# First mixer of a two-layer block: denser S5 tables, scans and rotations in fewer instructions, and a new order around them

## The chip, the cores and the metric

One Trainium2 chip, one core. The kernel runs a whole two-block network on 512 tokens of width 1024 in float32. The metric is the device time of one execution in microseconds; of several runs the median counts.

## The reference, cut to what matters

The first block has a mixer of two halves that share one projection, `proj = rms_norm(x) @ w_in`. The change lies in this mixer alone; what follows it (its feed-forward part, dilated attention, a squared-relu MLP, HGRN2 and another MLP) stays as it is.

```python
# S5: 32 groups of 16 inputs, 64 complex states each, over L = 512 steps
dt = exp(log_dt); mag = exp(lr * dt); ar, ai = mag * cos(li * dt), mag * sin(li * dt)
fr, fi = ((ar - 1) * lr + ai * li) / den, (ai * lr - (ar - 1) * li) / den
bbar_re, bbar_im = fr * b_re - fi * b_im, fr * b_im + fi * b_re
x[t] = (ar + i ai) * x[t-1] + bbar @ u[t]                 # associative_scan
y = einsum(xr, c_re) - einsum(xi, c_im) + d * u           # then gelu and a GLU
# attention: 8 query heads, 2 key heads of 64, window 128, sink
q, k = partial_rotary(q), partial_rotary(k)               # the first 16 of 64
# x1 * cos - x2 * sin, x2 * cos + x1 * sin, with x1, x2 of 8 each
```

## The kernel before, in words

**Arithmetic.** Every large product is made of three matmuls on split operands (`mm3`, L260 to L262): a weight tile of 128x1024 is loaded to `wst`, ACT copies its high part to `whi` (L183) and DVE subtracts to get `wlo` (L184). Splits are made ahead by `K.ws.more` and `take`. Every engine runs its instructions in the order in which the program emits them.

**S5 in chunks of four.** Time is cut into 128 chunks of 4 steps. A state has 64 values for each of two groups on the 128 partitions, and 16 such pairs of groups lie along the free axis. Four tables are made from the parameters: `tC`, `tS` (cosine and sine of 4m times the state's angle, m = 0 to 127) by doubling, n = 1, 2, ... 64, each doubling with a complex product (`cmul`, L945 to L950) and a squaring of the phase; `TP` (L996 to L1013: b times powers of a, the first half on DVE, the second on POOL); `CA` (L1024 to L1032: c times powers of a, on POOL). They are kept with zero blocks, so that a pair of groups is one matmul: b and c come from memory already padded from 16 to 32 columns, and every instruction on them runs over the zeros as well.

For each of four quarters f, `s5_in` multiplies the chunked inputs with `Pm` (transposed `TP`), rotates by the tables, runs eight scans of 128 elements on DVE (L1124) with the decay `r4` broadcast, and rotates back; DVE and POOL share these steps. `s5_kb` builds the part inside a chunk, `s5_y` the outputs, `s5_z` brings them back to the order of time with 32-column matmuls (L1171). `make_up` (L1048) is a similar rearrangement of the inputs.

**Attention.** `qkv` projects keys and values, then queries, in six pairs of token blocks. After each pair ACT evacuates and six DVE instructions rotate (L1220 to L1225), then PE transposes. `scores`, `normalize` and `values` follow.

**Order.** The angles (`angles`, L803 on) are emitted between the norms of the third and the fourth token block. Then come the splits of two u tiles, the u projection with the steps of `early` (TP, then tables) between its parts, and then the two strings `_MIX_INNER` and `_MIX_OUTER`, which list the remaining steps in order of emission: `e` a step of `early`, `CA0`/`CA1` a step of `make_CA`, `inF` of `s5_in`, `qkv`, `scT`, `yF`, `zF` and so on.

Of the kernel before, what the change touches and what calls it, by code (L numbers as in the profile page):

```python
# [210 lines left out]
_MIX_INNER = """e e CA0 e u qkv in0 qkv qkv in0 qkv in0 in1 qkv CA0 qkv in1 qkv Pm2 qkv CA0 CA0 in1 Pm3 qkv qkv qkv in2 in2  # L211
CA0 qkv xT in2 in3 kb0 qkv in3 sc0 qkv y0 CA1 sc1 sc0 CA1 CA1 sc0 sc1 in3 kb1 sc1 n0 tab v0 CA1 v0 n1 CA1 v0
# [16 lines left out]
class Kern:  # L229
# [573 lines left out]
    def angles(self, pool, th, n, cos, sin):  # L803

        K, nc = self, self.nc
        k = pool.tile([128, n], F32, name="ang_k")
# [7 lines left out]
        nc.scalar.activation(sin, th, AF.Sin)  # L814
        nc.scalar.activation(cos, k, AF.Sin)

    def mix(self, ctx):
# [25 lines left out]
        inv = load("c_inv8", [128, 8], q=G)  # L843
        get_xin(1)
# [5 lines left out]
        b_in = load("s5_b", [128, 2, 16, 32], pool)  # L850
        CAs, CI = [pool.tile([128, 2, 8, 5, 32], F32, name="CA")], {}

        def get_c(h, q):
            t = CI[h] = pool.tile([128, 2, 8, 32], F32, name="qk", bufs=3)
            q.dma_start(t, K.ins["s5_c"][:, :, 8 * h:8 * h + 8])

        get_c(0, nc.sync)
# [37 lines left out]
        G.tensor_tensor(dt, e16, prm[:, 2], op=OP.pow)  # L895
# [7 lines left out]
        G.tensor_scalar(lr, prm[:, 0], -1e-4, 0.0, op0=OP.min, op1=OP.add)  # L903
        G.tensor_mul(t16[0], lr, dt)
# [3 lines left out]
        square(3)  # L908
        V.tensor_copy(posf, pos_i)
# [3 lines left out]
        K.angles(c_, th, 48, cs[:, 0], cs[:, 1])  # L913
# [3 lines left out]

        prenorm(3)
# [34 lines left out]
        tb2 = K.xp.tile([128, 2, 16, 128], F32, name="x")  # L953
        tC, tS = tb2[:, 0], tb2[:, 1]
        e4 = [c_.tile([128, 16], F32, name=f"e4_{i}") for i in range(6)]
        ph = [[c_.tile([128, 16], F32, name=f"ph{n}_{i}") for i in range(2)] for n in range(2)]
        cmul(G, G, e4[0], e4[1], c1, s1_, c1, s1_, e4[2:])
        cmul(G, G, ph[0][0], ph[0][1], e4[0], e4[1], e4[0], e4[1], e4[2:])
# [3 lines left out]
        G.memset(tC[:, :, 0:1], 1.0)  # L962
        G.memset(tS[:, :, 0:1], 0.0)
        tmp = [pool.tile([128, 4, 128], F32, name=f"wt{i}") for i in range(4)]

        def tables():
            n = 1
            while n < 128:
                pr_, pi_ = ph[0]
                for o in range(0, n, 32):  # L970
                    w = min(n, 32)
                    bc = [p[:, :, None].to_broadcast([128, 16, w]) for p in (pr_, pi_)]
                    t = [t.rearrange("p a b -> p (a b)")[:, 0:16 * w].rearrange("p (g m) -> p g m", g=16) for t in tmp]
                    cmul(V, G if n > 4 else V, tC[:, :, n + o:n + o + w], tS[:, :, n + o:n + o + w],
                         tC[:, :, o:o + w], tS[:, :, o:o + w], bc[0], bc[1], t)
                    if n >= 16:
                        yield
                n *= 2
                if n < 128:
                    cmul(V, V, ph[1][0], ph[1][1], pr_, pi_, pr_, pi_, e4[2:])  # L980
                    ph.reverse()

        def b8(t, h):
            return t[:, None, 8 * h:8 * h + 8, None].to_broadcast([128, 2, 8, 32])

        TPs = {}

        def make_TP0():

            TP = TPs[0] = pool.tile([128, 2, 8, 4, 32], F32, name="TP")  # L990
            t1, t2 = (tmp[i].rearrange("p q (g m) -> p (q g) m", m=32).rearrange("p (c q) m -> p c q m", c=2)
                      for i in range(2))
            for j in (3, 2, 1, 0):
                a = b_in[:, :, 0:8] if j == 3 else TP[:, :, :, j + 1]
                yr, yi = (fr, fi) if j == 3 else (ar, ai)
                V.tensor_mul(t1, a, b8(yr, 0))  # L996
                V.tensor_mul(t2, a, b8(yi, 0))
                V.tensor_sub(TP[:, 0, :, j], t1[:, 0], t2[:, 1])
                V.tensor_add(TP[:, 1, :, j], t1[:, 1], t2[:, 0])
                yield  # L1000
            G.tensor_copy(b_in[:, :, 0:8], TP[:, :, :, 3])

        def make_TP1():

            TP = TPs[1]
            for j in (3, 2, 1, 0):
                a = b_in[:, :, 8:16] if j == 3 else TP[:, :, :, j + 1]
                yr, yi = (fr, fi) if j == 3 else (ar, ai)
                for c in range(2):
                    o = TP[:, c, :, j]  # L1010
                    G.tensor_mul(o, a[:, c], b8_(yr, 1))
                    G.tensor_mul(cat, a[:, 1 - c], b8_(yi, 1))
                    (G.tensor_add if c else G.tensor_sub)(o, o, cat)  # L1013
            G.tensor_copy(b_in[:, :, 8:16], TP[:, :, :, 3])

        cat = pool.tile([128, 8, 32], F32, name="cat")
        def b8_(t, h):
            return t[:, 8 * h:8 * h + 8, None].to_broadcast([128, 8, 32])

        def make_CA(h):  # L1020

            CA = CAs[h]
            c = CI.pop(h)
            G.tensor_copy(CA[:, 0, :, 0], c[:, 0])  # L1024
            G.tensor_scalar(CA[:, 1, :, 0], c[:, 1], -1.0, 0.0, op0=OP.mult, op1=OP.add)
            yield
            for n in range(4):
                for c in range(2):
                    o = CA[:, c, :, n + 1]
                    G.tensor_mul(o, CA[:, c, :, n], b8_(ar, h))  # L1030
                    G.tensor_mul(cat, CA[:, 1 - c, :, n], b8_(ai, h))
                    (G.tensor_sub if c else G.tensor_add)(o, o, cat)  # L1032
                yield
# [27 lines left out]
        def early():  # L1061
            yield from make_TP0()
# [12 lines left out]
        e = step(e)  # L1075
        K.transposes(xin[:, 3, :], xT, 3)
        e = step(e)
        u_half(2, 0)
        e = step(e)
        X = pool.tile([128, 2, 4, 4, 128], F32, name="X")  # L1080
        TPs[1] = X[:, :, 2:4].rearrange("p c f q (j h) -> p c (f q) j h", j=4)
        make_TP1()
# [54 lines left out]
        def s5_kb(f):  # L1137
# [5 lines left out]
            for q in range(4):  # L1143
                for j in range(4):
                    o = p[32 * j:32 * j + 32, q, 32 * j:128]
# [704 lines left out]
```

## Time and profile before

| | us |
|---|---|
| median of 3 runs (2193.4 to 2195.33) | 2195.24 |
| the profiled execution | 2195.75 |
| its span, first to last instruction | 2194.0 |
| PE busy in the span | 2117.1 (96%) |
| DVE busy | 1247.6 (57%) |
| ACT busy | 778.1 (35%) |
| POOL busy | 304.0 (14%) |

The span is the time from the first instruction to the last; the execution has 1.75 us around it. PE is the tensor engine, DVE the vector engine, ACT the scalar engine, POOL the general one. Shares over the whole span hide stages: the mixer takes roughly the first 300 us. A wait is idle time of an engine, put down to the instruction that ended it. The times of matmuls overlap, since they are pipelined; so do those of other engines by a little.

### The profile page before, as it was taken

How to read it: one execution, taken by the hardware profiler on the slowest of the kernel's cores; microseconds unless marked ns; L12 is line 12 of the kernel's file. 1: busy time of each engine (PE TensorE's matmuls, PEld its weight loads, DVE VectorE, ACT ScalarE, POOL GpSimd, SP SyncE). 2: the span in 40 equal slices, each digit the busy share in tenths (PEclk: the TensorE clock that was granted, in tenths of full speed). 3: DMA queues.
4: the chain of work that ended last, by engine and by line, in shares of the span. 5: the costliest groups of instructions: out<-in, count | busy, mean ns of one | idle time of the engine just before them, and what ended most of it. 6: DMA issues, size and time to landing. Idle time of an engine off the chain costs nothing.

```text
span 2194.0 us, 31487 instructions
## 1 busy us (share of the span) xinstructions
PE 2117.1 (96%) x12708; PEld 1772.8 (81%) x12708; DVE 1247.6 (57%) x2236; ACT 778.1 (35%) x1433; POOL 304.0 (14%) x366
## 2 busy tenths in 40 slices
PE   7779999999999999999999999999999999999997
PEld 6767788888888888888887888888898878888885
DVE  8986453334366666666666644444556556444444
ACT  4135443222223444424443433222254534322331
POOL 7660100000003212122220100000110001000001
PEclk9879999999999999999999999999999999999998
DMA  4200233223225333233332232223222222222321
GB/s 142 70 25 30 106 125 96 92 81 115 96 68 191 112 111 116 82 112 108 95 111 102 87 115 96 96 77 109 103 84 82 79 78 85 96 96 81 112 96 68
DMA packets 64994, 210.00 MB, mean 96 GB/s; under 512 B 10528, under 2 KB 15280, under 8 KB 64848
## 3 DMA queue, kind: packets, MB, share of 16 engines
q1 hardware_dynamic: 55808, 181.32, 24.4%
q0 software_dynamic: 6896, 20.08, 3.2%
q10 hardware_dynamic: 2144, 6.58, 0.9%
q8 instruction: 100, 1.64, 0.3%
q14 instruction: 46, 0.38, 0.1%
HBM read 186.97 MB, written 4.19 MB: 87 GB/s over the span
## 4 chain that ended last, share of the span: by engine, by line
PE 59%; issue 24%; DVE 2%; POOL 1%; ACT 1%; DMA 0%; POOLq 0%; ACTq 0%; DVEq 0%
PE mm L260 14%; PE mm L261 13%; PE mm L262 13%; PE dn L371 4%; PE dn L370 4%; PE dn L372 4%; PE o L734 1%; PE dn L657 1%; POOL rv L306 1%; POOL rr L308 1%; PE dn L711 1%; PE dn L713 1%; ACT P L641 0%; DVE wlo L184 0%; PE dn L744 0%
## 5 line engine op out<-in xcount | busy, mean ns | idle before, releaser
L260 PE MATMUL mm<-xh,whi 128*128 128x512 f32 (+1 forms) x1488 | 566.7, 381 | 3.0 <-ACT xh L312 3.0
L261 PE MATMUL mm<-xl,whi 128*128 128x512 f32 (+1 forms) x1488 | 558.1, 375 | 3.3 <-DVE xl L313 3.1
L262 PE MATMUL mm<-xh,wlo 128*128 128x512 f32 (+1 forms) x1488 | 557.5, 375 | 1.3 <-DVE wlo L184 1.3
L184 DVE TENSOR_TENSOR wlo<-wst,whi 128x1024 fp32r<-128x1024 f32 x328 | 441.2, 1378 | 130.4 <-ACT whi L183 129.5
L183 ACT ACTIVATE whi<-wst 128x1024 fp32r<-128x1024 f32 x328 | 331.7, 1049 | 372.0 <-PE dn L371 221.9
L260 PEld LDWEIGHTS mm<-xh,whi 128*128 128x128 f32 x1488 | 282.1, 190 | 60.9 <-issue 7.3
L262 PEld LDWEIGHTS mm<-xh,wlo 128*128 128x128 f32 x1488 | 282.3, 190 | 52.7 <-DVE wlo L184 1.5
L261 PEld LDWEIGHTS mm<-xl,whi 128*128 128x128 f32 x1488 | 282.3, 190 | 52.2 <-DVE xl L313 4.5
L371 PE MATMUL dn<-whi,hl 128*128 128x512 f32 x688 | 271.6, 395 | 0.0
L370 PE MATMUL dn<-whi,hh 128*128 128x512 f32 x688 | 271.0, 394 | 0.1
L372 PE MATMUL dn<-wlo,hh 128*128 128x512 f32 x688 | 268.6, 390 | 0.0
L260 PE MATMUL mm<-whi,xh 128*128 128x256 f32 x608 | 179.4, 295 | 4.5 <-DVE kT L1188 4.5
L261 PE MATMUL mm<-wlo,xh 128*128 128x256 f32 x608 | 173.8, 286 | 3.2 <-DVE wlo L184 3.2
L262 PE MATMUL mm<-whi,xl 128*128 128x256 f32 x608 | 173.6, 286 | 0.0
L480 DVE SCALAR_TENSOR_TENSOR x<-x,dn 128x512 f32<-128x512 f32 x112 | 75.6, 685 | 169.1 <-PE dn L372 169.1
L306 POOL TENSOR_SCALAR rv<-ss 128x1 f32<-128x1 f32 (+1 forms) x42 | 26.8, 638 | 1037.7 <-ACT junk L348 440.4
L370 PEld LDWEIGHTS dn<-whi,hh 128*128 128x128 f32 x688 | 129.4, 188 | 30.4 <-DVE x L341 0.5
L372 PEld LDWEIGHTS dn<-wlo,hh 128*128 128x128 f32 x688 | 129.4, 188 | 29.2
L371 PEld LDWEIGHTS dn<-whi,hl 128*128 128x128 f32 x688 | 129.6, 188 | 26.7
L260 PEld LDWEIGHTS mm<-whi,xh 128*128 128x128 f32 x608 | 118.1, 194 | 12.7 <-issue 7.5
L261 PEld LDWEIGHTS mm<-wlo,xh 128*128 128x128 f32 x608 | 118.4, 195 | 3.5 <-DVE wlo L184 3.4
L262 PEld LDWEIGHTS mm<-whi,xl 128*128 128x128 f32 x608 | 118.2, 194 | 0.0
(403 smaller groups left out, 2646.9 us busy)
## 6 DMA issues: line engine op xcount, KB each, us to landing
wst<-in_wstream SPq DMA_DIRECT2D x328, 512.0 KB, 3.5
qks<-qkT POOLq DMA_DIRECT2D x96, 128.0 KB, 2.7
v<-gb SPq DMA_DIRECT2D x128, 32.0 KB, 1.8
X<-in_x SPq DMA_DIRECT2D x4, 512.0 KB, 7.7
xn<-in_x POOLq DMA_DIRECT2D x4, 512.0 KB, 4.6
x_d<-x POOLq DMA_DIRECT2D x4, 512.0 KB, 8.9
x<-x_d POOLq DMA_DIRECT2D x4, 512.0 KB, 7.4
out<-x SPq DMA_DIRECT2D x4, 512.0 KB, 2.6
```

Source lines behind the costliest of these rows:

```text
L183: K.nc.scalar.activation(hi, t, AF.Copy)
L184: K.nc.vector.tensor_sub(lo, t, hi.bitcast(F32))
L260: mm(ps, wh, xh, start=first, stop=False, skip_group_check=True)
L261: mm(ps, wh, xl, start=False, stop=False, skip_group_check=True)
L262: mm(ps, wl, xh, start=False, stop=last, skip_group_check=True)
L306: self.nc.gpsimd.tensor_scalar(v[:, :n], ss, scale, eps, op0=OP.mult, op1=OP.add)
L308: self.nc.gpsimd.tensor_tensor(r[:, :n], v[:, :n], self.nhalf[:, :n], op=OP.pow)
L370: mm(p, hT[i][0][:, c], w[i][0][:, n], start=i == 0, stop=False)
L371: mm(p, hT[i][1][:, c], w[i][0][:, n], start=False, stop=False)
L372: mm(p, hT[i][0][:, c], w[i][1][:, n], start=False, stop=i == m - 1)
L480: nc.vector.scalar_tensor_tensor(x, x, ALPHA if first else 1.0, ps, op0=OP.mult, op1=OP.add)
L657: mm(s, q[r, 0, c], q[r, 1, keys], start=True, stop=True)
```

## The change

- b and c come unpadded (16 columns). `TP` is made for both halves at once on DVE in a small buffer, and ACT copies each power into the padded tables; `CA` stays on POOL with half the elements, and ACT copies it at the end. The padded tables are zeroed by memsets first.
- The tables for m = 0 to 15 and the phases 64, 128 and 256 come from angles directly: one product with a constant, one call of `angles` on 16x19 elements, and Sin on ACT. Only n = 16, 32 and 64 are doubled.
- The norms of all four blocks now come first; POOL's power for dt, and all angles, follow.
- `s5_in` runs two scans of 512 elements, with a decay table `R_tab` (made by ACT) that has zeros where a new row of 128 begins.
- The rotation takes four instructions instead of six, with a table `rot` that ACT fills (its sine part once negated).
- `s5_kb` and `s5_z` emit their matmuls so that successive ones write different groups of 32 columns.
- `_MIX_INNER` is reordered: `CA0` has three steps instead of five and its two large ones stand around the first step of `in0`; `CA1` has three, from the same place on.

```diff
-_MIX_INNER = """e e CA0 e u qkv in0 qkv qkv in0 qkv in0 in1 qkv CA0 qkv in1 qkv Pm2 qkv CA0 CA0 in1 Pm3 qkv qkv qkv in2 in2
-CA0 qkv xT in2 in3 kb0 qkv in3 sc0 qkv y0 CA1 sc1 sc0 CA1 CA1 sc0 sc1 in3 kb1 sc1 n0 tab v0 CA1 v0 n1 CA1 v0
+_MIX_INNER = """R e e e u qkv CA0 in0 qkv CA0 qkv in0 CA0 qkv in0 in1 qkv qkv in1 qkv Pm2 qkv in1 Pm3 qkv qkv qkv in2 in2
+qkv xT in2 in3 kb0 qkv in3 sc0 qkv CA1 y0 sc1 sc0 CA1 sc0 sc1 in3 kb1 sc1 CA1 n0 tab v0 v0 n1 v0
...
-        b_in = load("s5_b", [128, 2, 16, 32], pool)
+        mult = load("c_mult", [128, 19], q=G)
+        V.memset(TPs[0], 0.0)
+        V.memset(b_in, 0.0)
+        G.memset(CAs[0], 0.0)
...
         square(3)
+        prenorm(3)
+        G.tensor_tensor(dt, e16, prm[:, 2], op=OP.pow)
...
+        V.tensor_mul(th2, th[:, 0:16, None].to_broadcast([128, 16, 19]), mult[:, None].to_broadcast([128, 16, 19]))
+        K.angles(k2, th2, [((slice(None), slice(None), slice(0, 16)), tC[:, :, 0:16], tS[:, :, 0:16]),
+                           ((slice(None), slice(None), slice(16, 19)), ph[:, 0], ph[:, 1])])
+        rot = c_.tile([128, 2, 4, 2, 8], F32, name="rot")
+        A.activation(rot[:, 0], rc[:, :, None].to_broadcast([128, 4, 2, 8]), AF.Copy)
+        A.activation(rot[:, 1, :, 0], rs, AF.Copy, scale=-1.0)
+        A.activation(rot[:, 1, :, 1], rs, AF.Copy)
...
         def tables():
-            n = 1
-            while n < 128:
+            for i, n in enumerate((16, 32, 64)):
...
+        def make_TP():
+            roll = K.gp.tile([128, 2, 2, 16, 16], F32, name="gb")
+            a = b_raw
             for j in (3, 2, 1, 0):
+                V.tensor_mul(t1, a, yr)
+                V.tensor_mul(t2, a, yi)
+                a = roll[:, j % 2]
+                V.tensor_sub(a[:, 0], t1[:, 0], t2[:, 1])
+                V.tensor_add(a[:, 1], t1[:, 1], t2[:, 0])
+                for h in range(2):
+                    for g in range(2):
+                        r, c = slice(64 * g, 64 * g + 64), slice(16 * g, 16 * g + 16)
+                        A.activation(TPs[h][r, :, :, j, c], a[r, :, 8 * h:8 * h + 8], AF.Copy)
...
         def make_CA(h):
+            for n in range(4):
                 for c in range(2):
+                    o = d[:, c, :, n]
+                    G.tensor_mul(o, a[:, c], arb)
+                    G.tensor_mul(cat, a[:, 1 - c], aib)
                     (G.tensor_sub if c else G.tensor_add)(o, o, cat)
+                if n % 2:
+                    yield
+            for g in range(2):
+                r, k = slice(64 * g, 64 * g + 64), slice(16 * g, 16 * g + 16)
+                A.activation(CAs[h][r, :, :, 0, k], c0[r], AF.Copy)
+                A.activation(CAs[h].rearrange("p c q n h -> p (c q) n h")[r, :, 1:5, k],
+                             d.rearrange("p c q n h -> p (c q) n h")[r], AF.Copy)
+            yield
+        def factors(f):
+            if f == 0:
+                R_tab.append(K.gp.tile([128, 2, 4, 128], F32, name="gb"))
+                G.memset(R_tab[0][:, :, :, 0:1], 0.0)
+            A.activation(R_tab[0][:, f % 2, :, 1:128], r4[:, 4 * f:4 * f + 4, None].to_broadcast([128, 4, 127]), AF.Copy)
...
         u_half(1, 0)
-        e = step(e)
         K.transposes(xin[:, 3, :], xT, 3)
+        X = pool.tile([128, 2, 4, 4, 128], F32, name="X")
+        G.memset(X[:, :, 2:4], 0.0)
         e = step(e)
         u_half(2, 0)
         e = step(e)
-        make_TP1()
+        e = step(e)
         u_half(0, 1)
...
             for y in (xr, xi):
-                for q in range(4):
-                    V.tensor_tensor_scan(y[:, q], r4[:, 4 * f + q:4 * f + q + 1].to_broadcast([128, 128]), y[:, q], 0.0,
-                                         op0=OP.mult, op1=OP.add)
+                y = y.rearrange("p q m -> p (q m)")
+                V.tensor_tensor_scan(y, R, y, 0.0, op0=OP.mult, op1=OP.add)
...
+                for c in range(2):
+                    for j in range(4):
+                        mm(p[32 * j:32 * j + 32, q, 32 * j:128], bb[:, c, q],
+                           CA[:, c, f4 + q, 0:4 - j].rearrange("p n h -> p (n h)"), start=c == 0, stop=c == 1)
...
-            for q in range(4):
-                for i in range(4):
+            for i in range(4):
+                for q in range(4):
                     mm(p[32 * q:32 * q + 32, i, :], K.ident[:, 32 * i:32 * i + 32], yt[:, q, :], start=True, stop=True)
...
-                    V.tensor_mul(q4[0], x1, cb)
-                    V.tensor_mul(q4[1], x2, sb)
-                    V.tensor_mul(q4[2], x2, cb)
-                    V.tensor_mul(q4[3], x1, sb)
-                    V.tensor_sub(x1, q4[0], q4[1])
-                    V.tensor_add(x2, q4[2], q4[3])
+                    V.tensor_mul(q4[0], x, cb)
+                    V.tensor_mul(q4[1][:, :, :, 0:8], x[:, :, :, 8:16], sb[:, :, :, 0:8])
+                    V.tensor_mul(q4[1][:, :, :, 8:16], x[:, :, :, 0:8], sb[:, :, :, 8:16])
+                    V.tensor_add(x, q4[0], q4[1])
```

## Rows read from the trace of the kernel before

**Rows 1.** The page's slices, DVE: busy tenths in 40 equal slices.
```profile
DVE  8986453334366666666666644444556556444444
```
**Rows 2.** Stretches: length, busy us of each engine, granted clock, DMA share, GB/s.
```profile
43.60:72.50 28.90, 25.70 (x238) 23.93 (x229) 28.86 (x78) 10.00 (x16) 17.75 (x21) 0.94 0.23 78
72.50:137.75 65.25, 44.89 (x366) 42.80 (x364) 64.28 (x108) 12.60 (x21) 44.59 (x43) 0.82 0.16 53
...
160.00:190.00 30.00, 28.55 (x328) 24.03 (x326) 18.89 (x68) 19.01 (x46) 0.00 (x0) 0.94 0.00 1
```
**Rows 3.** PE's waits in 0 to 300 us: total, times, longest.
```profile
PE mm L1184 <- DVE qk L1225: 11.7, 3, 5.7
```
**Rows 4.** DVE in order of time: start, us, line, operation, shapes.
```profile
11.41 1.22 DVE L184 TENSOR_TENSOR wlo<-wst,whi 128x1024 fp32r<-128x1024 f32 x1
...
42.07 1.63 DVE L184 TENSOR_TENSOR wlo<-wst,whi 128x1024 fp32r<-128x1024 f32 x1
43.62 0.58 DVE L945 TENSOR_TENSOR wt<-x,ph 128x16 f32<-128x16 f32 x1
...
53.73 0.42 DVE L945 TENSOR_TENSOR wt<-x,ph 128x256 f32<-128x256 f32 x1
...
57.17 0.16 DVE L945 TENSOR_TENSOR e<-ph 128x16 f32<-128x16 f32 x1
...
58.31 1.53 DVE L946 TENSOR_TENSOR wt<-x,ph 128x512 f32<-128x512 f32 x1
59.77 0.68 DVE L947 TENSOR_TENSOR wt<-x,ph 128x512 f32<-128x512 f32 x1
```
**Rows 5.** POOL in order of time, beside the second last of these.
```profile
57.81 1.49 POOL L948 TENSOR_TENSOR wt<-x,ph 128x512 f32<-128x512 f32 x1 [1.65 <-DVE ph L950]
```
**Rows 6.** The instructions on wt in TP's four steps, summed: DVE is third.
```profile
sum 13.40, PE 0.00 PEld 0.00 DVE 13.05 ACT 0.00 POOL 0.00; mean PE 0.00 PEld 0.00 DVE 4.35 ACT 0.00 POOL 0.00
```
**Rows 7.** POOL in order of time, at the powers.
```profile
16.58 2.91 POOL L920 TENSOR_TENSOR mag<-e,t 128x16 f32<-128x16 f32 x1
```
**Rows 8.** PE in order of time, with the wait ahead, at the second u tile.
```profile
23.86 0.39 PE L262 MATMUL mm<-xh,wlo 128*128 128x256 f32 x1 [1.27 <-DVE wlo L184]
```
**Rows 9.** ACT's groups by form: count, busy us, mean ns, idle time before.
```profile
L1173 ACT ACTIVATE x<-mm 128x512 fp32r<-128x512 f32 x4 | 4.3, 1084 | 5.6 <-PE mm L1171 5.6
...
L1281 ACT ACTIVATE PT<-dn 128x512 f32<-128x512 f32 x4 | 2.4, 592 | 5.1 <-PE dn L1278 5.1
...
L1212 ACT ACTIVATE v<-mm 128x256 f32<-128x256 f32 x2 | 0.8, 378 | 0.0
```
**Rows 10.** The scans' line L1124 alone by stretches: length, DVE busy us.
```profile
85.00:100.00 15.00, 6.12 (x8) 0.77 0.01 3
...
sum 60.00, DVE 17.21; mean DVE 4.30
```
**Rows 11.** DVE's groups by form, the scan of the HGRN stage.
```profile
L1579 DVE TENSOR_TENSOR_SCAN b<-reset,sg 128x512 f32<-128x512 f32 x8 | 9.8, 1220 | 13.8 <-ACT sg L1576 13.8
```
**Rows 12.** The rotation's instructions (those on junk), 80 to 130 us: DVE busy, ACT busy.
```profile
80.00:130.00 50.00, 14.67 (x36) 0.00 (x0) 0.80 0.15 48
```
**Rows 13.** DVE in order of time, two instructions of the rotation.
```profile
101.28 0.21 DVE L1221 TENSOR_TENSOR junk<-qk,cs 128x64 f32<-128x64 f32 x1
...
105.29 0.65 DVE L1221 TENSOR_TENSOR junk<-qk,cs 128x64 f32<-128x64 f32 x1
```
**Rows 14.** POOL's groups by form, a product of 128 elements.
```profile
L948 POOL TENSOR_TENSOR wt<-x,ph 128x128 f32<-128x128 f32 x1 | 0.5, 512 | 1.7 <-DVE ph L949 1.7
```
**Rows 15.** DVE in order of time, two normalisations of eight products.
```profile
152.97 3.76 DVE L1265 TENSOR_SCALAR xh<-xh,aL 128x256 f32<-128x256 f32 x8
...
198.51 2.19 DVE L1265 TENSOR_SCALAR xh<-xh,aL 128x256 f32<-128x256 f32 x8
```
**Rows 16.** PE in order of time, two rearrangements with 32 columns each.
```profile
50.40 1.95 PE L1048 MATMUL dn<-u,ident 128*32 128x128 f32 x64
...
177.13 2.46 PE L1171 MATMUL mm<-wt,ident 128*32 128x128 f32 x32
```

More of the change, by code (lines that the diff above doesn't have):

```diff
@@ L800, in attn, with angles @@
         self.xT = self.xT_next
-    def angles(self, pool, th, n, cos, sin):
+    def angles(self, k, th, outs):
         K, nc = self, self.nc
-        k = pool.tile([128, n], F32, name="ang_k")
         nc.vector.tensor_scalar(k, th, 1.0 / (2 * math.pi), 12582912.0, op0=OP.mult, op1=OP.add)
@@ L849, in mix @@
         K.ws._load()
-        b_in = load("s5_b", [128, 2, 16, 32], pool)
[L851 to L857, printed above, removed]
+        tmp = [pool.tile([128, 4, 128], F32, name=f"wt{i}") for i in range(4)]
+        b_raw, t1, t2 = (tmp[i].rearrange("p a (b h) -> p (a b) h", h=16).rearrange("p (c q) h -> p c q h", c=2)
+                         for i in (2, 0, 1))
+        nc.sync.dma_start(b_raw, K.ins["s5_b"])
+        c_raw = {0: pool.tile([128, 2, 8, 16], F32, name="qk", bufs=3)}
+        nc.sync.dma_start(c_raw[0], K.ins["s5_c"][:, :, 0:8])
+        b_in = pool.tile([128, 2, 16, 32], F32, name="bb")
+        CAs = [pool.tile([128, 2, 8, 5, 32], F32, name="CA")]
+        TPs = [pool.tile([128, 2, 8, 4, 32], F32, name="TP")]
+        V.memset(TPs[0], 0.0)
+        V.memset(b_in, 0.0)
+        G.memset(CAs[0], 0.0)
         def wa(*labels, **kw):
@@ L961, in mix @@
         G.tensor_mul(r4, r4, r4)
-        G.memset(tC[:, :, 0:1], 1.0)
-        G.memset(tS[:, :, 0:1], 0.0)
-        tmp = [pool.tile([128, 4, 128], F32, name=f"wt{i}") for i in range(4)]
         def tables():
-            n = 1
-            while n < 128:
-                pr_, pi_ = ph[0]
+            for i, n in enumerate((16, 32, 64)):
                 for o in range(0, n, 32):
                     w = min(n, 32)
-                    bc = [p[:, :, None].to_broadcast([128, 16, w]) for p in (pr_, pi_)]
+                    bc = [ph[:, c, :, i:i + 1].to_broadcast([128, 16, w]) for c in range(2)]
@@ L1016, in mix @@
[L1016 to L1025, printed above, removed]
-            yield
[L1027 to L1033, printed above, removed]
+                    yield
@@ new lines, in mix, with make_CA @@
+        cat = pool.tile([128, 8, 16], F32, name="cat")
+        R_tab = []
+        def make_CA(h):
+            q = slice(8 * h, 8 * h + 8)
+            arb, aib = (t[:, q, None].to_broadcast([128, 8, 16]) for t in (ar, ai))
+            d = K.gp.tile([128, 2, 8, 4, 16], F32, name="gb")
+            c0 = c_raw.pop(h)
+            G.tensor_scalar(c0[:, 1], c0[:, 1], -1.0, 0.0, op0=OP.mult, op1=OP.add)
+            for n in range(4):
+                a = d[:, :, :, n - 1] if n else c0
+                for c in range(2):
+                    o = d[:, c, :, n]
+                    G.tensor_mul(o, a[:, c], arb)
+                    G.tensor_mul(cat, a[:, 1 - c], aib)
+                    (G.tensor_sub if c else G.tensor_add)(o, o, cat)
+                if n % 2:
+                    yield
+            for g in range(2):
+                r, k = slice(64 * g, 64 * g + 64), slice(16 * g, 16 * g + 16)
+                A.activation(CAs[h][r, :, :, 0, k], c0[r], AF.Copy)
+                A.activation(CAs[h].rearrange("p c q n h -> p (c q) n h")[r, :, 1:5, k],
+                             d.rearrange("p c q n h -> p (c q) n h")[r], AF.Copy)
+            yield
@@ L1061, in early @@
         def early():
-            yield from make_TP0()
+            yield from make_TP()
             yield from tables()
@@ L1322, in mix @@
         parts.update({f"v{t}": values(t, inner_pt) for t in range(2)})
-        calls = {"u": free_u, "xT": free_xT, "tab": free_tables}
+        calls = {"R": lambda: [factors(f) for f in range(2)], "u": free_u, "xT": free_xT, "tab": free_tables}
         calls.update({f"Pm{f}": partial(make_Pm, f) for f in (2, 3)})
@@ L1804, in layout @@
     d["c_inv8"] = np.ascontiguousarray(np.broadcast_to(inv8, (128, 8)))
+    d["c_mult"] = np.ascontiguousarray(np.broadcast_to(
+        np.array([4 * m for m in range(16)] + [64, 128, 256], np.float32), (128, 19)))
     d["positions"] = np.ascontiguousarray(a["positions"][0].reshape(4, 128).T)
```

97 lines of the change are left out of this document (32 added, 65 removed).

## The prediction, made blind

> **What bounds the kernel now.** I read the page's slices first: in the first three (55 us each) DVE is 80 to 90% busy, a share it never reaches again [rows 1]. So the stage to look at is the first mixer. The stretches show it closer: from 43.6 to 72.5 us DVE is busy 28.86 of 28.9 us, from 72.5 to 137.75 us 64.28 of 65.25, while PE has 44.89 busy us in the latter, at a mean granted clock of 0.82 [rows 2]. PE's longest wait names the releaser: 11.7 us for the rotated heads of DVE's L1225 [rows 3]. Up to the scores, then, what DVE no longer has to do shortens the program, as long as PE, ACT and POOL follow. After 160 us PE is busy 28.55 of 30 us [rows 2] and only PE's own work counts.
>
> A second reading decides the prices. The same product of 512 elements takes DVE 0.68 us (L947) or 1.53 (L946); the long one starts while POOL's L948 (57.81, 1.49 us) runs and ends with it [rows 4, 5]. DVE and POOL block each other for whole instructions, so taking work from POOL is also worth something on DVE.
>
> **The change, part by part: up to the end of the tables (72.5 us before).**
> - Doubling steps n = 1, 2, 4, 8 fall: from 43.62 to 53.73 us DVE does nothing else [rows 4], -10.1. Two later squarings go too, six instructions of 16 elements each (the first at 57.17): -1.1 at some 0.09 apart [rows 4]. In their place come nine instructions on 304 elements; one of 256 takes 0.42 us [rows 4], and an instruction starts 0.08 before the one ahead of it ends (42.07 + 1.63 against 43.62), so about 0.4 each: +3.6 (bounds 3.0 and 4.5, as if some met POOL).
> - TP. Before, DVE builds the padded half: 13.05 us [rows 6], and POOL the other half beside it. Dense, both halves are again 512 elements per product, without POOL: two products of 0.68 and two sums of 0.42 (256 elements), less the overlap, make 1.9 us a step, 7.5 for four: -5.5. Four weight splits among them lose their collisions too (1.63 us, the first one 1.22 [rows 4]): about -1.5.
> - The angles move behind the norms. POOL's power for dt no longer stands ahead of the third norm's factor, which gives PE's first projection some 0.7 us. But it now starts behind the last norm's factor, where the second power stood (16.58, 2.91 us [rows 7]), and DVE's product with dt (L912) waits for it: until about 19.6, where DVE, by its durations, is free at 18: +1.6. On POOL the second power, r4 and the memset of X queue behind it, and nobody waits for these yet. Queued behind that wait are all angles, the 14 small instructions and then the splits of the second and third u tile. [...]
> - ACT's scatter. Each TP step adds four copies of 256 elements on 64 partitions; one of 256 elements takes 0.38 us [rows 9], 0.3 without the overlap: 1.2 us a step, after the sums on DVE. Behind them on ACT stand the high parts of the next weight tiles, and for these waits DVE's low part: after the third step 1.2 + 0.5 (u's copy) + 1.05, after the fourth 1.2 + 1.0: +5.0 (bounds 0, if they are hidden, and 9 at the stretched price below).
> - The memsets of TP, b and CA lie before 7 us, where DVE and POOL wait for x: nothing. ACT's rot and factor copies (about 0.3 and 0.6 us) fill idle time of ACT.
> Sum here: -18.2 + 14.1 = -4.1.
>
> **Up to the scores (72.5 to 137.75 us).**
> - Scans: 32 of 128 elements cost 17.21 us, one group of eight 6.12 of it beside POOL's CA work [rows 10]. A scan of 512 elements takes 1.22 us in the later HGRN stage [rows 11]; eight make 9.8: -7.4 (bound -5.0, if that group would have been like the others anyway).
> - Rotary: 36 instructions, 14.67 us [rows 12]. One of 64 elements takes 0.21 alone, 0.65 beside POOL [rows 13]. Four instructions of 64 to 128 elements need about 0.75 a time, 0.55 for k: 4.1; with some collisions left 5.5: -9.2 (bounds -10.6 and, if each still meets POOL, 0).
> - Six weight splits at about 1.7 us beside POOL (1.63 in rows 4), against 1.22 alone: -2.9.
> - POOL: CA of 128 instead of 256 elements. The nearest row has 0.51 us for 128 elements [rows 14]; less the overlap 24 instructions make about 11 us. They now stand on POOL ahead of in0's difference and products, in0's last sum there frees the buffers of in1's products, and ACT's scatter of CA holds the next head's copy. I follow POOL from 68 us: two halves of CA at 5.4 with in0's subtraction between, then 1.3 + 1.3 + 1.7; in1 can start at 83.5 to 87.5 where DVE would be free at 79.6: +6 (bounds 4 and 11).
> Sum: -19.5 + 6 = -13.5, leaving 51.8 us; PE's 44.9 us still fit.
>
> **Behind it.** The second normalisation (eight products, 3.76 us beside POOL, 2.19 without [rows 15]) comes after the shorter CA1: -1.6. S5 outputs: s5_z's 32 instructions take 2.46 us when four in turn go to the same 32 columns; make_up's 64, which change columns each time, 1.95 [rows 16]. In turn a tile therefore costs about 1.0: -1.2 for each of the first three, which stand on PE's path; the fourth is followed by ACT's exponentials, which its evacuation waits for anyway: nothing. -3.6 (bounds 0 and -5.4). s5_kb already changes columns after every second matmul, and its longest column has two matmuls of 128 elements for each q in either order: I take nothing (bound: half of what s5_z gains, on the two of four that stand on PE's path, -1.2).
>
> Total -4.1 - 13.5 - 5.2 = -22.8 on the profiled execution of 2195.75 us (span 2194.0, 1.75 around it), which lies 0.5 above the median of the runs, 2195.24: 2172.
>
> A rule against the scatter: ACT writing 512 elements four apart takes 1084 ns, an ordinary evacuation 592 [rows 9]. [...] I take the plain price; the other stands in the range.
>
> **The rivals.**
> - *Better: the new waits are hidden.* If DVE's waits for ACT and PE (5.0 + 3.9) and half the wait for POOL disappear, -12 more: 2160. For it: ACT is busy only 10.00 of 28.9 us [rows 2]. Against: both chains are in program order, with nothing queued on DVE that could go first.
> - *The block between DVE and POOL stays.* Fewer elements, but CA's instructions are as many, and each DVE instruction that meets one waits for it. Then the rotary gains 0 instead of 9.2 and CA costs 5 more: 2172 + 14 = 2186. For it: the 0.65 of 64 elements is the length of POOL's instruction, not DVE's. Against: in the new order CA0 is done before three quarters of the rotary work. [...]
> - *Part of it does nothing:* column tiles in turn bring no overlap. 2172 + 3.6 = 2176, inside the forecast's own range.
> [...]
>
> **How the numbers follow.** Forecast 2172 with its own range 2165 to 2180: 0.52. Hidden waits, 2157 to 2165: 0.17. The block stays, 2180 to 2189: 0.20. No change to be seen (waits and block together, about 2194): 0.05. Slower by the clock: 0.06. The range 2157 to 2188 leaves out the last two and a little more. A change of 0.2% (4.4 us) is about what a measurement of this kernel can tell from none. Faster 0.89, same 0.05, slower 0.06.
>
> **What would show it.** Tables: no 16-element products on DVE, the end of the n = 64 step near 68 us. Rotary: instructions of 64 and 128 elements at 0.2 to 0.3 us; if they stand at 0.6, the second rival holds. Scans near 1.2 us. Scores (L1249 before) begin near 120 us. A PE wait of some 6 us for wlo near 22 us, and DVE waits for ACT's whi between 40 and 50 us. s5_z at about 1.0 us. The prediction is wrong if scores begin before 112 or after 132 us, or if anything behind 300 us differs.

## The result, and the profile after

| | before | after |
|---|---|---|
| median, first comparison (4 runs each) | 2194.32 | 2181.22 |
| ratio, 95% interval | | 0.9943 [0.9929, 0.9958] |
| median, timed again beside two other kernels (9 and 5 runs) | 2194.71 | 2185.77 |
| ratio, 95% interval | | 0.9961 [0.9948, 0.9973] |
| span of the profiled execution | 2194.0 | 2179.2 |

The change makes the kernel faster by 13.1 us in the first comparison and by 8.9 in the second. 22.8 were forecast. The direction is right and the size is not. The two comparisons of the same kernel differ by 4.2 us; the section on the experiments shows where in the execution that arises. All times below are compared with runs of the kernel before on the same chip.

Where the gain arises, read from the starts of instructions in both traces (us from the span's start):

| | before | after | difference |
|---|---|---|---|
| end of the n = 64 table step | 72.50 | 71.07 | -1.4 |
| in1's first product on DVE | 88.51 | 93.36 | +4.9 |
| in2's first product | 114.16 | 111.82 | -2.3 |
| scores, first instruction on DVE | 137.75 | 133.13 | -4.6 |
| from there to the last normalisation | 60.76 | 53.35 | -7.4 |
| from there to the end | 1995.5 | 1992.7 | -2.8 |

So two thirds of the profiled gain lie behind the scores, where the prediction had a quarter. The stretches of the kernel after, in the columns of [rows 2]; the third is that from scores to the last normalisation:

```profile
43.60:71.07 27.47, 23.20 (x264) 20.98 (x265) 21.62 (x25) 17.64 (x30) 9.72 (x9) 1.00 0.29 101
71.07:133.13 62.06, 50.10 (x422) 47.83 (x421) 53.86 (x72) 18.14 (x29) 42.93 (x43) 0.89 0.16 54
133.13:186.48 53.35, 44.89 (x556) 34.96 (x557) 37.92 (x137) 36.26 (x101) 10.95 (x26) 0.90 0.03 10
```

and the last one in the kernel before:

```profile
137.75:198.51 60.76, 54.49 (x553) 43.93 (x554) 40.88 (x137) 33.93 (x97) 17.14 (x27) 0.83 0.03 10
```

DVE lost 10.4 busy us between tables and scores (64.28 to 53.86) and the stretch only 3.2. Against [rows 1] the page's slices say the same: DVE's first three slices are 6, 8 and 7 tenths now.

```profile
DVE  6876443333466666657766744444556556444444
```

What stands in the place of DVE's work are waits. PE's and DVE's longest, from 50 to 137 us (line and what it waited for: total, times, longest):

```profile
PE mm L1191 <- ACT v L1219: 4.6, 1, 4.6
...
DVE X L1138 <- POOL wt L1134: 3.7, 1, 3.7
DVE wlo L184 <- ACT whi L183: 2.9, 1, 2.9
DVE X L1132 <- POOL X L1128: 2.8, 1, 2.8
```

PE's 11.7 us for the rotation [rows 3] have become 2.3; in their place PE stands 4.6 us for ACT's copy of v, and ACT waits for POOL. In order of time, POOL and then ACT:

```profile
72.27 1.27 POOL L1016 TENSOR_SCALAR qk<-qk 128x128 f32<-128x128 f32 x1
...
74.84 0.40 POOL L1022 TENSOR_TENSOR cat<-qk,ai 128x128 f32<-128x128 f32 x1
...
80.76 1.29 POOL L1128 TENSOR_TENSOR X<-wt,wt 128x512 f32<-128x512 f32 x1
...
82.38 1.32 POOL L1022 TENSOR_TENSOR cat<-gb,ai 128x128 f32<-128x128 f32 x1
...
88.74 1.26 POOL L1134 TENSOR_TENSOR wt<-X,x 128x512 f32<-128x512 f32 x1
```

```profile
88.81 1.06 ACT L1029 ACTIVATE CA<-gb 64x1024 f32<-64x1024 f32 x1 [14.81 <-POOL gb L1023]
...
91.55 0.38 ACT L1219 ACTIVATE v<-mm 128x256 f32<-128x256 f32 x1
```

CA0 keeps POOL from 72.27 to 88.74, in0's subtraction (L1128) in its middle. A product of 128 elements takes 0.40 us beside DVE's first four products of in0 (74.54 to 77.01) and 1.32 where it meets a scan (82.09). ACT has queued its copies of CA0 ahead of v and so reaches v at 91.55.

### The profile page after: what moved, and what is told of

The parts are those of the page before. It is cut to its first block, busy times and chain, and to the rows that moved or that the text cites. A ratio compares the mean times of both kernels' runs of the same rounds, so it can differ in the third digit from the quotient of the medians.

```text
span 2179.2 us, 31391 instructions
## 1 busy us (share of the span) xinstructions
PE 2102.1 (96%) x12708; PEld 1758.0 (81%) x12708; DVE 1223.5 (56%) x2153; ACT 794.0 (36%) x1470; POOL 272.3 (12%) x327
## 4 chain that ended last, share of the span: by engine, by line
PE 59%; issue 24%; DVE 2%; POOL 1%; ACT 1%; DMA 0%; POOLq 0%; ACTq 0%; DVEq 0%
PE mm L260 14%; PE mm L261 13%; PE mm L262 13%; PE dn L371 4%; PE dn L370 4%; PE dn L372 4%; PE o L734 1%; PE dn L657 1%; POOL rv L306 1%; POOL rr L308 1%; PE dn L711 1%; PE dn L713 1%; ACT P L641 0%; DVE wlo L184 0%; PE dn L744 0%
```

## The experiments

Theories at the start, for the part of the gain that is missing: **A**, POOL's order (CA0 ahead of in0); **B**, the late start of PE's projections; **C**, DVE stops being the bound as soon as it is relieved. From the first four runs came **D**, that DVE and POOL hold each other per POOL instruction, and from the next four **G**, that three queues (DVE, ACT, PE) end the stretch together. Medians, each with the kernel before on the same chip and the ratio's interval:

| kernel | median | before | less by | ratio | scores at |
|---|---|---|---|---|---|
| splits early | 2184.73 | 2194.47 | 9.7 | [0.9939, 0.9966] | 133.00 |
| CA0 late | 2189.25 | 2194.47 | 5.2 | [0.9973, 0.9991] | 136.82 |
| before + local parts | 2190.00 | 2194.47 | 4.5 | [0.9974, 0.9991] | 135.82 |
| after - local parts | 2189.25 | 2194.47 | 5.2 | [0.9969, 0.9988] | 133.23 |
| s5_in on DVE | 2186.38 | 2194.18 | 7.8 | [0.9953, 0.9978] | 135.49 |
| before + column tiles | 2191.12 | 2194.18 | 3.1 | [0.9980, 0.9998] | 137.72 |
| after - column tiles | 2187.70 | 2194.18 | 6.5 | [0.9960, 0.9983] | 132.48 |
| CA0's copies later | 2185.71 | 2194.18 | 8.5 | [0.9950, 0.9977] | 133.46 |
| two moves | 2181.31 | 2194.71 | 13.4 | [0.9924, 0.9949] | 129.93 |
| after, again | 2185.77 | 2194.71 | 8.9 | [0.9948, 0.9973] | 133.36 |
| three moves | 2180.37 | 2194.71 | 14.3 | [0.9926, 0.9953] | 128.85 |
| two moves, short scans | 2183.59 | 2193.21 | 9.6 | [0.9935, 0.9962] | 131.75 |

**Splits early.** The splits of the u tiles ahead of the wide angles:

```diff
+        wu = wa(*[("u", f) for f in range(3)], ahead=0)
         tb2 = K.xp.tile([128, 2, 16, 128], F32, name="x")
...
-        wu = wa(*[("u", f) for f in range(3)], ahead=0)
```

> The changed kernel with one move: the splits of the second and third u tile are emitted ahead of the 304-element angles. Theory A (the missing 9 us were lost to POOL: CA0's two halves lie around in0's first step) expects no change, 2180 to 2182 us, since DVE does the same work up to the end of the tables. Theory B (they were lost at the start: PE stood 5.8 us for the second whi and began qkv 10.3 us later than before) expects the 5.8 us wait of PE to shrink below 1 us, the first qkv matmul to come from 62.5 to about 57 us, and 3 to 6 us less in all: 2175 to 2178 us.

PE's wait of 5.8 us for whi shrinks to 1.2 and the tables end 1.6 us earlier, but in2 begins at 111.68 and scores at 133.00, as in the kernel after (111.82, 133.13): DVE waits 2.23 us for PE ahead of in2 instead of 0.74. B falls: a start that is 1.6 us earlier is worth nothing at scores as long as something else ends there.

**CA0 late.** c's raw half is loaded into a u buffer, and CA0's steps stand behind in1:

```diff
-R e e e u qkv CA0 in0 qkv CA0 qkv in0 CA0 qkv in0 in1 qkv qkv in1 qkv Pm2 qkv in1 Pm3 qkv qkv qkv in2 in2
+R e e e u qkv in0 qkv qkv in0 qkv in0 in1 qkv qkv in1 CA0 qkv Pm2 qkv in1 CA0 Pm3 qkv CA0 qkv qkv in2 in2
...
```

> The changed kernel with CA0's three steps behind both steps of in1, and its source loaded late into a u buffer, so that POOL meets in0 and in1 with nothing ahead. Theory A (POOL's order) expects DVE's waits of 2.8 and 3.7 us and PE's 4.6 us wait for v to go, in0's first sub right behind its products, and scores some 5 us earlier: 4 to 7 us less in all, 2174 to 2177 us. Theory B (late start of PE) expects 2180 to 2182 us. If kb0 then waits for CA0, both gain and loss show in that one wait.

Both waits of DVE for POOL went, and in1 began at 85.33 instead of 93.36, 6.9 us earlier beside the 1.2 by which in0 already was: A has its gain there. Then all of it was lost, on DVE and on ACT, in order of time:

```profile
114.73 0.29 DVE L1224 TENSOR_TENSOR junk<-qk,rot 128x128 f32<-128x128 f32 x1 [11.77 <-ACT qk L1216]
```

```profile
111.65 1.06 ACT L1028 ACTIVATE CA<-gb 64x1024 f32<-64x1024 f32 x1 [11.66 <-POOL gb L1022]
...
114.10 0.60 ACT L1216 ACTIVATE qk<-mm 128x512 f32<-128x512 f32 x1
```

ACT's copies were emitted right behind the build, ahead of a head's copy, and ACT works in order. The edit put the fault of the change at a worse place. As a test of the total it decides nothing; as one of the mechanism it shows both halves.

**Local parts alone, and without them.** Before with 8 scans, 4 rotary operations and the column tiles in turn; after with these three undone, dense tables and order kept:

> The kernel before with the three local parts alone: 8 long scans, 4 rotary operations, S5 outputs by column tiles in turn (kb too); the tables, their order and the doubled build stay. The sum of the prediction gives them 7.4, 9.2 and 3.6 us: 20.2 us less, 2174 us. If DVE stops being the bound as soon as it is relieved (theory C: in the stretch of the scans PE or POOL ends last), it is less: 10 to 14 us, 2180 to 2184 us.

> The changed kernel with the three local parts undone: 32 scans of 128, 6 rotary operations, S5 outputs by the same column tile; the dense tables, the angles and the new order stay. The sum of the prediction gives these 2.6 us (4.1 and 2.9 and 1.6 gained, 6 lost): about 2192 us. Theory A and theory B, by which this part lost some 9 us more, expect about 2200 us; theory C, by which the parts are worth little once the other is there, expects it near the kernel before or under it, 2188 to 2194 us.

4.5 and 5.2 us: together 9.7, within what the whole change measured. So the parts add up, as far as these intervals tell. The tables and the order are no loss, as A and B had it, but worth 5.2 us (interval 2.6 to 6.8) where the sum had 2.6; 2189.25 lies in C's range. The local parts fell short, 4.5 in place of 20.2, and below the 10 to 14 that C left them. Scores come at 133.23 without them and at 133.13 with them. Rotary instructions (those on junk) in the kernel after, in after without the local parts, in before with them, and in before with the column tiles alone, whose rotation is the old one: stretch, length, DVE busy us and count, clock:

```profile
80.00:125.00 45.00, 7.87 (x24) 0.89 0.15 50
```

```profile
80.00:125.00 45.00, 8.91 (x36) 0.89 0.15 50
```

```profile
80.00:130.00 50.00, 16.01 (x24) 0.80 0.15 48
```

```profile
80.00:130.00 50.00, 14.67 (x36) 0.78 0.15 49
```

Beside the old build 24 instructions take longer than 36, 16.01 against 14.67; beside the dense one 36 need 8.91 already, and 24 save 1.04. What a rotation costs is set mainly by the POOL instructions that it meets, and little by its own number.

The scans do get shorter, and the products behind them longer. In in2, the kernel without the local parts and the kernel after:

```profile
114.60 3.69 DVE L1124 TENSOR_TENSOR_SCAN X<-r,X 128x128 f32<-128x128 f32 x8
118.22 0.66 DVE L1129 TENSOR_TENSOR wt<-X,x 128x512 f32<-128x512 f32 x1
118.80 1.74 DVE L1130 TENSOR_TENSOR wt<-X,x 128x512 f32<-128x512 f32 x1
```

```profile
115.20 2.34 DVE L1132 TENSOR_TENSOR_SCAN X<-gb,X 128x512 f32<-128x512 f32 x2
117.45 1.70 DVE L1136 TENSOR_TENSOR wt<-X,x 128x512 f32<-128x512 f32 x1
119.08 1.74 DVE L1137 TENSOR_TENSOR wt<-X,x 128x512 f32<-128x512 f32 x1
```

The scans save 1.36 us. But POOL's two products also need them; with short scans the first ran beside the second four scans, now both meet DVE's, and 1.04 us goes back: net 0.33, by the starts of the sum (6.05 against 5.72). In in0 the saving turns into waiting: DVE waits 2.8 and 3.7 us for POOL there, and 1.5 and 2.4 without the local parts. In the kernel before with the local parts the stretch to the scores shows the whole account:

```profile
72.50:135.80 63.30, 44.27 (x366) 42.19 (x364) 62.19 (x72) 13.70 (x23) 49.40 (x43) 0.84 0.17 54
```

DVE has 36 instructions fewer than in [rows 2] and its scans cost 10.03 instead of 17.21 us, yet it is busy 62.19 us instead of 64.28, without a wait, and POOL's 43 instructions grew from 44.59 to 49.40. That is D.

**s5_in on DVE.** All twelve elementwise instructions of a tile on DVE:

```diff
-            G.tensor_sub(xi, tmp[2], tmp[3])
+            V.tensor_sub(xi, tmp[2], tmp[3])
...
-            G.tensor_mul(tmp[2], xr, s)
-            G.tensor_mul(tmp[3], xi, c)
+            V.tensor_mul(tmp[2], xr, s)
+            V.tensor_mul(tmp[3], xi, c)
...
-            G.tensor_add(xi, tmp[2], tmp[3])
+            V.tensor_add(xi, tmp[2], tmp[3])
```

> The changed kernel with all twelve elementwise instructions of s5_in on DVE: POOL's sub, two products and add of each tile move there. Theory D (a POOL instruction holds the two-input DVE instruction that it meets for about its own length, whichever it is, so POOL's half of a tile saves DVE nothing) expects per tile four more DVE instructions at a pitch of 0.60 us, +2.4 us, against what goes: waits of 2.8 and 3.7 us and a 1.74 us add in in0 (-7.6), 2.1 us of the wlo pair beside in1's products, 2.2 us in the products of in2 and of in3. Sum 9.6 - 14.1 = -4.5 us at scores, 133.1 to about 128.6 us, and 2175 to 2178 us in all. By the prediction's own accounting, in which POOL's half is help, it is +9.6 - 6.5 = +3 us: 2184 us.

The total, 2186.38, is neither, and scores come at 135.49, 2.4 us later: nearer to the +3 of the prediction's accounting than to the -4.5 of D. On DVE it went as D says up to there: with four more instructions in0 ends at 86.5 instead of 91.8, and the wlo pair beside in1 takes 2.34 us instead of 4.47. But then:

```profile
91.76 0.23 DVE L1225 TENSOR_TENSOR junk<-qk,rot 128x64 f32<-128x64 f32 x1 [5.29 <-ACT qk L1217]
...
98.33 2.34 DVE L184 TENSOR_TENSOR wlo<-wst,whi 128x1024 fp32r<-128x1024 f32 x2
```

DVE waits 5.29 us for the same queue on ACT, and ahead of in2 another 2.6 for PE; from 119 us on CA1, for which POOL is now free, stretches DVE's instructions: the last six of in3 take 0.77 to 0.94 us instead of 0.68. The collisions went as D has them, and its forecast of 4.5 us failed.

**Column tiles alone, and without them.**

> The kernel before with the S5 outputs (and kb) by column tiles in turn and nothing else. By the prediction's sum this is worth 3.6 us: 2190.9 us. The three local parts together measured 2190.0 us, so theory D (scans and rotary give next to nothing while POOL builds beside DVE) expects this run at 2190 to 2191 us, and the scans and rotary operations worth under 1 us there. If the column tiles are worth under 2 us by themselves (2192.5 us or more), the scans and rotary operations have the rest.

> The changed kernel with the S5 outputs and kb in the old order of column tiles, nothing else undone. The prediction's sum expects +3.6 us: 2184.8 us, and scores unchanged at 133.1 us. With all three local parts undone it was 2189.25 us and scores came at 133.2 us, so theory D expects the scans and rotary operations to be worth under 1.5 us here, and this run at 2187.5 to 2189.5 us: the column tiles would be worth 6 to 8 us, their own 3 to 4 and as much again in stretches at the full clock behind scores.

3.1 us alone (interval 0.4 to 4.4); in the trace of that run the stretch from scores to the last normalisation is 56.75 us instead of 60.76. Without them the kernel after gains 6.5 us in place of 8.9: 2.4 us. The 6 to 8 that D gave them there, from the first 2181 us of the kernel after, were too many, and 2187.70 lies in its range by luck. Against the runs with all three local parts on or off, scans and rotary together are left with 1.4 us (4.5 - 3.1) and 1.3 us (6.5 - 5.2). That is the number for the 16.6 us of the prediction; each of the four gains behind it is known to about 2 us, so it says small and no more.

**CA0's copies later.** One token moved:

```diff
-R e e e u qkv CA0 in0 qkv CA0 qkv in0 CA0 qkv in0 in1 qkv qkv in1
+R e e e u qkv CA0 in0 qkv CA0 qkv in0 qkv in0 in1 qkv CA0 qkv in1
...
```

> The changed kernel with CA0's third step, ACT's copies, two qkv steps later, so that ACT evicts v and qk before it waits for POOL; POOL's own order stays. Theory A in its second form (the loss is ACT standing 14.8 us behind POOL, and PE 4.6 us behind ACT) expects PE's wait of 4.6 us for v to go and 3 to 5 us less in all: 2176 to 2178 us. Theory D expects PE's wait to go too, but the end to stay, since DVE is busy 98% from 92 to 133 us and sets when scores begin: 2180 to 2182 us, scores at 132 to 133.5 us.

PE no longer waits for v, and waits for the rotation instead:

```profile
PE mm L1191 <- DVE qk L1228: 7.4, 2, 5.9
```

2185.71 us, which is what the kernel after gave when it was timed again; scores come at 133.46, as D has it. The total is above D's 2180 to 2182, which were counted from the first 2181. ACT's standstill was real, and DVE behind POOL hid it.

**Two moves, three moves, and the kernel after again.** Tiles 0 and 1 of s5_in on DVE (tiles 2 and 3 as they are) with the copies later; then the early splits too:

> The changed kernel with two moves at once: s5_in of tiles 0 and 1 wholly on DVE (tiles 2 and 3 keep POOL's half), and ACT's copies of CA0 two qkv steps later. Alone, the first let DVE reach the end of in0 at 86.4 instead of 91.7 us and then stand 5.3 us for ACT, the second freed ACT and left DVE late. Theory G (three queues, DVE, ACT and PE, end this stretch within a microsecond or two of each other, so relief of one shows as a wait of another) expects both waits to go together: in1 to begin near 88 instead of 93.4 us, in2 at 105 to 108 instead of 111.8, scores at 127 to 130 instead of 133.1, and 2176 to 2179 us in all. [...]

> Both moves of the run before, and the splits of the second and third u tile ahead of the 304-element angles as well, which by themselves brought the first qkv matmul and the end of the tables 1.6 us forward and nothing at scores. Theory G expects the 1.6 us to come through now: in2 1 to 2 us ahead of the kernel with the two moves, and as much less in all. Its rival (PE and its clock end the stretch) expects in2 where the kernel with two moves has it, within 0.5 us.

Two kernels begin scores no later than the kernel after and end 3.5 and 6.5 us above the median of its first runs (splits early, 133.00 and 2184.73; after - column tiles, 132.48 and 2187.70).

> The changed kernel as it is, once more, beside the two others on one chip: 2181 us by its first runs. [...] If that difference belongs to the kernels, this run gives 2180 to 2182 us again; if it was the draw of the first runs, 2183 to 2186 us.

Together the moves work: in1 begins at 88.68, in2 at 108.62, scores at 129.93, and the time is 4.5 us under that of the kernel after beside it on the same chip, 3.4 of them by the start of scores. DVE's rows at the two places, with its remaining wait, now for PE:

```profile
87.45 0.42 DVE L1226 TENSOR_TENSOR junk<-qk,rot 128x64 f32<-128x64 f32 x1
...
94.65 2.33 DVE L184 TENSOR_TENSOR wlo<-wst,whi 128x1024 fp32r<-128x1024 f32 x2
...
108.62 0.69 DVE L1125 TENSOR_TENSOR wt<-dn,x 128x512 f32<-128x512 f32 x1 [2.56 <-PE dn L1121]
```

In2 came half a microsecond after the 105 to 108 expected, since PE is next (DVE waits 2.56 us for it), and 3.2 us before that of the kernel after (111.82). The time lies above 2176 to 2179, which were counted from the first 2181. With the third move it begins at 107.19, 1.4 us earlier, as G expects; of the 1.1 us at scores the time shows 0.9, less than the measurement tells apart. Both kernels beat the kernel before. Their runs, 2177.71 to 2182.33 us, lie below those of the kernel after beside them (2184.74 to 2186.42) but not below its first four (2180.92 to 2184.06); they are the best found, and the runs don't tell them apart.

The repeated kernel gave 2185.77 us, 4.55 more than at first, with the same waits and scores at 133.36. What differs is where the clock is granted. A stretch ahead of the second normalisation, and 30 us far behind the mixer, in the repeated run:

```profile
139.30:142.70 3.40, 3.10 (x45) 2.18 (x37) 2.10 (x9) 2.52 (x12) 3.17 (x10) 0.50 0.00 0
1755.00:1785.00 30.00, 26.75 (x202) 21.38 (x201) 17.97 (x39) 8.21 (x24) 1.20 (x2) 0.94 0.09 30
```

and both in the first profile of the kernel after:

```profile
139.30:142.70 3.40, 1.96 (x40) 1.31 (x36) 2.14 (x8) 3.30 (x14) 3.24 (x9) 1.00 0.00 0
1755.00:1785.00 30.00, 26.60 (x206) 20.64 (x206) 18.70 (x43) 8.20 (x24) 2.40 (x4) 1.00 0.02 7
```

The second normalisation starts at 148.34 instead of 147.13, and from the last one to the end it takes 1995.2 instead of 1992.7 us. This last piece is the same code in every kernel here and varied from 1992.6 to 1996.0 us over the fourteen profiles; the mean of 0.94 in these 30 us stands against 1.00 in the other profile. Over the nine runs of this kernel the time goes with the mean granted clock of the execution: 2180.92 to 2181.39 us at 0.988 or 0.989, 2184.06 at 0.987, 2184.74 to 2186.42 at 0.986. So of the first 13.1 us about 4 were probably not the change's own: the two profiles differ by 3.8 us, 3.6 of them behind the scores.

**Two moves with short scans.** The prediction's two large terms, once more, where the waits are gone: 32 scans of 128 and 6 rotary operations in the kernel with two moves.

> The kernel with the two moves (tiles 0 and 1 wholly on DVE, CA0's copies later; 2181.31 us) with 32 scans of 128 and 6 rotary operations in place of 8 and 4. The prediction's terms for these two, 7.4 and 9.2 us, would make it about 2198 us, scores at 146 us in place of 129.9. Theory D, by which these terms were collisions with POOL and a count of the wrong thing, prices a tile's scans at 1.36 us (3.70 against 2.34) where DVE meets no POOL product behind them, which is tiles 0 and 1 here, 0.3 us in tiles 2 and 3, and the six rotations at 0.15 us each: 4.2 us on DVE. Of that PE, for which DVE waits 2.6 us ahead of in2, hides most of the 3.1 us up to there. Scores at 130.5 to 132 us and 2182 to 2184 us in all.

Scores at 131.75, 1.8 us later, and 2183.59 us, 2.3 more by the medians, lie inside D's numbers; by the distance to the kernel before it is 3.8, above them. All are far from 16.6. D's price for the scans, 1.36 us a tile, was too high all the same. In in1 of these two kernels POOL does nothing beside DVE (from 87.5 and from 90.0 us to beyond 110). There eight short scans, and in the kernel with two moves two long ones, take:

```profile
93.04 2.63 DVE L1125 TENSOR_TENSOR_SCAN X<-r,X 128x128 f32<-128x128 f32 x8
```

```profile
92.39 2.34 DVE L1133 TENSOR_TENSOR_SCAN X<-gb,X 128x512 f32<-128x512 f32 x2
```

So the long scans themselves save 0.3 us a tile. The other 1.07 of the 3.70 are the collision with POOL's first product, which the long scans hand on to the products behind them.

## Why the prediction was right in direction and wrong in size

| step | predicted | found |
|---|---|---|
| to the end of the tables | -4.1 | -1.4 in the trace |
| scans | -7.4 | -7.5 busy on their line; with the rotary -1.3 to -3.8 in time |
| rotary | -9.2 | -6.8 busy, of it 5.8 from the dense build and order |
| six splits between tables and scores | -2.9 | 0.0 |
| CA0 ahead of in0 | +6 | +6.9, by in1's start without it |
| second normalisation | -1.6 | -1.57 |
| column tiles of s5_z | -3.6 | -3.1 timed, -4.0 in the trace |
| s5_kb | 0 | 0 |

**What failed** is the step that prices scans and rotary as DVE time: instructions removed, times their mean. The 14.67 us of [rows 12] and the 17.21 of [rows 10] were read as costs of these instructions. About half of the first (36 of them take 7.38 us in the kernel with two moves and short scans) and 6.7 us of the second (four tiles at 2.63 make 10.5) were collisions with POOL's instructions, charged to whichever DVE instruction met them. By rows without POOL the edit itself saves 0.3 us a tile on the scans and 0.14 on each of six rotations, an estimate of 2.0 us for the 16.6 forecast; 1.3 to 3.8 were measured, by which comparison is taken. The prediction had this in hand: it says that the two "block each other for whole instructions", and its second rival puts the rotary at 0 and 2186 us. It gave that case 0.20 because it argued from where CA0 would lie, and not from POOL's total beside DVE (44.59 us before, 42.93 after, in a stretch of 62). Both medians, 2181.22 and 2185.77, lie in that rival's 2180 to 2189 and outside the forecast's own 2165 to 2180. The outer range, 2157 to 2188, holds them only because it takes in that rival. And the rival's sum came out partly by luck: it left the scans at 7.4 and let CA0 cost 11, while the scans gave next to nothing and CA0 cost 6.9. The price per rotary instruction was also taken from one pair of rows: 0.65 beside POOL and 0.21 alone [rows 13], without asking whether a collision is avoided by having fewer of them. One reading is off: the long product of [rows 4] doesn't end with POOL's L948 [rows 5] but 0.54 us behind it, at 59.84 against 59.30, as if it had gone on once POOL was done.

**The splits** between tables and scores show the same: 10.4 us before and after, one pair of them 4.47 beside in1's products and another 2.35.

```profile
L184 DVE TENSOR_TENSOR wlo<-wst,whi 128x1024 fp32r<-128x1024 f32 x6 | 10.4, 1767 | 0.0
```

**POOL's CA0** was costed rightly in kind and nearly in size, at 6.9 where 6 was taken and 4 to 11 allowed. The chain the prediction followed (halves around the subtraction, in0's last sum, ACT's scatter ahead of a head's copy) is the chain in the trace; the halves took 8.5 us (with the negation ahead of the first) and 6.7 in place of 5.4, since POOL's instructions that meet DVE's splits and scans take 1.26 to 1.36 us.

**Up to the tables** the signs hold but for the splits. The angle instructions on 304 elements take 0.32 to 0.52 us (predicted 0.4), PE waits 5.8 us for the second u tile (6), DVE 0.93 for dt (1.6), 4.00 for the late transposes (3.9), and TP's four steps take 8.9 us (7.5). No run shows the 3.9 in the prediction's 14.1 as such; in its place the kernel after has these 4.00, behind PE's wait of 5.76 us and a granted clock of 0.50 from 27 to 33 us, which is 1.00 again at 33.5. DVE in order of time:

```profile
21.48 0.32 DVE L806 TENSOR_SCALAR wt<-wt 128x304 f32<-128x304 f32 x1
...
34.61 1.29 DVE L313 TENSOR_TENSOR xl<-dn,xh 128x512 fp32r<-128x512 f32 x2 [4.00 <-ACT xh L312]
...
46.52 1.22 DVE L184 TENSOR_TENSOR wlo<-wst,whi 128x1024 fp32r<-128x1024 f32 x1 [3.87 <-ACT whi L183]
...
60.06 4.31 DVE L184 TENSOR_TENSOR wlo<-wst,whi 128x1024 fp32r<-128x1024 f32 x2
```

Too small was ACT's scatter: 1.7 us a step instead of 1.2, so DVE waited 6.7 us for whi (3.87 and a later 2.85) in place of 5.0. The splits among these steps were to lose collisions worth 1.5 us and lost none in sum, 8.4 us before and 8.5 after: two fell to 1.22 and 1.23, but a pair took 4.31 instead of 3.42 beside POOL's table sum, memsets and product. With TP's 1.4 and 0.4 for the angles that makes 5.1 us; the shorter wait for dt gives 0.7 back and the doublings that stay 1.3, which leaves 3.1 for the 2.7 that are missing. The tables end 1.4 us earlier, and yet the kernel without the local parts gains 5.2: its scores come at 133.23 instead of 137.75, so POOL's smaller build and the order pay behind the tables, not ahead of them.

**Behind the scores** the mechanism held. The normalisation and two of the s5_z tiles, on DVE and PE:

```profile
147.13 2.19 DVE L1268 TENSOR_SCALAR xh<-xh,aL 128x256 f32<-128x256 f32 x8
```

```profile
158.58 1.08 PE L1178 MATMUL mm<-qk,ident 128*32 128x128 f32 x32
...
167.03 1.08 PE L1178 MATMUL mm<-wt,ident 128*32 128x128 f32 x32
```

1.08 where 2.46 stood [rows 16], 1.0 predicted. Of the 7.4 us there the tiles have 4.0 and the normalisation 1.6; for the other 1.8 the mean clock, 0.90 against 0.83, is the nearest cause, which no run shows by itself; the repeated run took 1.1 of them back. The prediction's sign that "anything behind 300 us differs" did appear, 2.8 us from the last normalisation to the end, and the repeated run, 1995.2 us there against 1995.5 before, shows that it belongs to the execution and not to the change.

**What would show it.** Scores at 133 lie outside the 112 to 132 that the prediction set, so it named its own failure; the rotary at 0.2 to 0.3 us was seen where POOL rests (0.28 at 103.25) and 1.29 to 1.36 where it doesn't; the prediction had named 0.6 as the mark of the second rival. The slower outcome by the clock did not come: the 0.50 behind PE's wait ended at 33 us, and the stretch to the scores has 0.89 against 0.82. Hidden waits did not come either. What neither the sum nor a rival had is that DVE, ACT behind POOL, and PE end the stretch so close together that each relief alone stayed within 1.1 us of the kernel after (9.7, 8.5 and 7.8 against 8.9) and brought scores no earlier than 133.00, and two together gave 4.5 and scores at 129.93.

Not tried is the late CA0 with its copies late as well; that it would gain is a guess from the two runs that hold its halves. Why a given execution gets its stretches at a granted clock of 0.50 where it does stays open.

## What to carry to other kernels

An instruction that is long because another engine holds it is priced by the holder (in the kernel after L1225 took 1.29 us at 91.69 beside POOL's sum of 1.60, and 0.28 at 103.25, where POOL rests): count POOL's instructions beside DVE, and before crediting a saving on DVE ask whether that count falls. Copies that wait for a build on another engine belong, on an in-order queue, just ahead of their reader and behind every eviction that is due earlier; here ACT stood 14.81 us for POOL with v's copy queued behind. Where relief of one engine turns up as a wait of another, try the moves together before dropping them, and time the winner again: here two comparisons of one kernel differ by 4 us.

## What was not expected of the hardware

- Four products of DVE kept their time beside POOL. In the kernel after, L1124 to L1127 of in0, which have one operand in dn, written by PE, keep a pitch of 0.60 us and take 0.67 to 0.68 us each, while POOL's CA0 runs beside them at 0.40 us a product (74.84 above):

```profile
75.14 0.68 DVE L1125 TENSOR_TENSOR wt<-dn,x 128x512 f32<-128x512 f32 x1
```

- Where DVE works beside POOL's short instructions, CA0's in the kernel after (0.90 and 0.95) or CA1's with s5_in on DVE (0.77 to 0.94), its own of 512 elements take 0.77 to 0.95 us instead of 0.68; beside one long POOL product in in2, 1.70 to 1.74.
- ACT's copies of 256 elements onto 64 partitions take 0.42 us each and follow each other without overlap, 0.85 a pair:

```profile
38.37 0.85 ACT L1000 ACTIVATE TP<-gb 64x256 f32<-64x256 f32 x2 [3.30 <-DVE gb L996]
```
